# Opening a feed-forward stage with two plain pairs, with the sums of x on VectorE

## The chip, the cores and the metric

The program runs on one core of a Trainium2 chip. The metric is the device time of one execution in microseconds. It is Bass code under the Tile framework: Tile places the buffers and semaphores and orders the instructions of each engine by its own timeline, except inside `strict()` (L102), where TensorE, VectorE and ScalarE instructions keep the order in which the program writes them. GpSimd's do not.

## The reference, cut to what matters

Two layers over 1024 prompt and 32 sample tokens (1056 columns) with model width 1024 and inner width 2816, all in float32. Layer 0 is a gated convolution mixer and layer 1 is attention; each is followed by this feed-forward block, which the change touches:

```python
def _conv_ffn(h, ctx, w_up, conv_w, w_down):
    up = h @ w_up                                  # 1024 -> 2 * 2816
    upc, new_ctx = _causal_dwconv(up, ctx, conv_w) # width 3, along the tokens
    g, v = jnp.split(upc, 2, axis=-1)
    return (jax.nn.silu(g) * v) @ w_down, new_ctx  # h = rmsnorm(x), x is added after
```

## The kernel before, in words

Tokens lie along the free dimension, channels on the 128 partitions: x is 8 tiles of 128 x 1056. A float32 product is made of three passes on TensorE with fp32r operands: each operand is split into a high part (ScalarE copy) and a low part (VectorE subtraction), and high*high, high*low and low*high are summed in PSUM. One matmul has 264 columns.

A feed-forward stage (`ffn`, L811) makes 22 pairs of 128-channel units, g and v of the same channels. From pair 2 on a pair goes by Strassen-Winograd (`pair`, L729): the 1024 x 256 weight and the two halves of the tokens are cut in blocks, and seven products of 24 matmuls (168) take the place of eight (192). It needs sums of the weight blocks (`ws`, four GpSimd operations a pair), the blocks of x named "11", "21" and "22", and the sums of x named t1 to t4, each four tiles with high and low part. Evictions are ScalarE copies and VectorE additions. After each pair `act` does the convolution: per unit a ScalarE product and two VectorE taps, then silu, the product of both and its split (`last`). From pair 3 on, the down projection of two finished pairs is streamed between the products (`stream`, L882).

The opening of a stage is written in strict order. `tokenwise` (L354) ends the stage before, normalising x in four column pieces (ENDS); the last piece's scalings are left to `begin`. `begin` (L531) makes pair 0 plainly, in two halves of the tokens, 96 matmuls each over eight steps, and splits the blocks of x on the way. After each step `tick` runs functions that are due at that step (`at`) and then jobs in order while their costs fit the room (`job`). In the second half it starts the sums: `first` and `second` make them in place in x, one half of each on VectorE and one on GpSimd; t1 to t3 have their low parts from VectorE, t4 from GpSimd. Pair 1 is then a Strassen pair of its own (`first_pair`, L775) whose seven products wait for t1 to t4 in turn, while the convolution of pair 0 is put in as jobs. Then all that is left is emitted, with the whole convolution of pair 1, and Tile's order begins with pair 2. The whole opening happens twice, once per layer.

Buffers: `slot` (14 in a stage), `keep` (24), `w` (4 weight operands), `wr` (5 raw weight blocks), and PSUM banks "p" (3) for the pairs and "d" (2) for the stream.

Of the kernel before, what the change touches and what calls it, by code (L numbers as in the profile page):

```python
# [12 lines left out]
F32 = mybir.dt.float32  # L13
# [15 lines left out]
PAD = 2  # L29
# [12 lines left out]
NF = DFF // 128  # L42
NP = HEADS // 2
SLOTS = 20
UPSLOTS = 14
# [40 lines left out]
class Net:  # L86
# [267 lines left out]
    def tokenwise(self, weight, acts, x, scale, units=(), lag=False):  # L354
# [16 lines left out]
        for c in ENDS:  # L371
# [19 lines left out]
            for k in range(3):  # L391
                self.at(3 + k, lambda f=steps: next(f))
            if c is ENDS[-1]:
                self.norm = scale(c, out[:, cs])
            else:
                for f in scale(c, out[:, cs]):
                    self.job(f, 0.45, 9 if c is ENDS[-2] and units else 7)
# [133 lines left out]
    def begin(self, x, early, late):  # L531
# [5 lines left out]
        one, two = (slice(*c) for c in HALVES)  # L537
        orders = tuple(range(NK)), tuple(k + i for k in range(k2) for i in (0, k2))

        def made(n, k, src, engine=None):  # L540
            def high():
                near = n in ("t2", "t4") or n == "t3" and k < 2
                t = b[n][k] = (self.keep if near else self.slot)("b", [128, 2, HB], F32R)
                self.nc.scalar.activation(t[:, 0], src, AF.Copy)

            def low():
                t = b[n][k]
                (engine or self.nc.vector).tensor_sub(t[:, 1], src, t[:, 0].bitcast(F32))

            return high, low  # L550

        def first(k):
            p, q = x[k], x[k + k2]
            self.nc.vector.tensor_sub(p[:, one], p[:, two], p[:, one])
            self.nc.gpsimd.tensor_sub(p[:, two], q[:, two], p[:, two])

        def second(k):
            q = x[k + k2]
            self.nc.vector.tensor_sub(q[:, two], q[:, two], x[k][:, one])
            self.nc.gpsimd.tensor_sub(q[:, one], q[:, two], q[:, one])  # L560

        t1 = [made("t1", k, x[k][:, one]) for k in range(k2)]
        t2 = [made("t2", k, x[k + k2][:, two]) for k in range(k2)]
        t3 = [made("t3", k, x[k][:, two]) for k in range(k2)]
        t4 = [made("t4", k, x[k + k2][:, one], self.nc.gpsimd) for k in range(k2)]
        for i in range(2):
            c = HALVES[i]
            ps = [self.bank("p").rearrange("p (q c) -> p q c", q=2) for _ in us]
            for n, m in enumerate(orders[i]):
# [16 lines left out]
                if i and n == 4 or not i and n == 0:  # L586
                    next(early)
                self.tick(0.4 if i == 0 or n < 2 else 0.7)
                if i and n % 2:
                    k = n // 2  # L590
                    self.job(lambda k=k: first(k), 0.7)
                    self.job(t1[k][0], 0)
                    if k:
                        self.job(t1[k - 1][1], 0.7)
            for u, p in zip(us, ps):
# [6 lines left out]
        self.ready = []  # L602
        self.job(t1[-1][1], 0.7, label="t1")
        for k in range(k2 + 1):
            if k < k2:
                self.job(lambda k=k: second(k), 0.7)
                self.job(t2[k][0], 0)
            if k:
                self.job(t2[k - 1][1], 0.7, label="t2")
        order = (2, 3, 0, 1)  # L610
        for k, last in zip(order + (None,), (None,) + order):
            if k is not None:
                self.job(t3[k][0], 0)
            if last is not None:
                self.job(t3[last][1], 0.7, label="t3")
        todo = late(us)
        todo = iter([todo[i] for i in (0, 4, 1, 2, 3, 5, 6, 7)])
        for k in range(k2 + 1):
            if k < k2:
                self.job(t4[k][0], 0)  # L620
            if k:
                self.job(t4[k - 1][1], 0, label="t4")
                cost, f = next(todo)
                self.job(f, cost)
        for cost, f in todo:
            self.job(f, cost)
        return b, us

# [145 lines left out]

    def first_pair(self, top, low, b, us):  # L775

        todo = self.pair(top, low, b, us)
        later = todo[4][3]
        todo = [todo[i] for i in (0, 4, 2, 1, 3, 5, 6)]
        for i in (3, 4):  # L780
            todo[i][0]()
        yield
        for _, operand, _, _ in todo[:2]:
            operand(True)
        yield
        for i, (_, _, product, evict) in enumerate(todo):
            self.until({1: "t1", 3: "t2", 4: "t3", 5: "t4"}.get(i))
            product()
            self.tick(1.4)
            if i + 2 < len(todo):  # L790
                if i + 3 == len(todo):
                    todo[-1][0]()
                todo[i + 2][1]()
            if i != 1:
                evict()
            if i == 4:
                later()
            yield

    def late(self, dst, src, ps):  # L800

        for d, q, s in self.cuts():
            self.nc.vector.tensor_add(dst[:, d], src[:, q, s], ps[:, q, s])

    def first(self, l):

        return [self.a["w_up"][l, i] for i in (0, NF)]

    def ffn(self, l, x, done):
# [4 lines left out]
        def act(t, g, v):  # L814

            y = {}

# [5 lines left out]
            def last():  # L823
# [3 lines left out]
                for d, p in spread((0, TT), PAD, PAD):  # L827
                    self.nc.scalar.activation(h[:, d], y[1][:, p], AF.Copy)
                    self.nc.vector.tensor_sub(low[:, d], y[1][:, p], h[:, d].bitcast(F32))  # L829
                acts.append((h, low))  # L830

            todo = ((1.0, lambda: taps(0, g, t)),
                    (1.3, lambda: self.taps(y[0], g, cw[:, t], 1)),
                    (1.3, lambda: self.taps(y[0], g, cw[:, t], 2)),
                    (0.3, lambda: self.nc.scalar.activation(y[0], y[0], AF.Silu)),
                    (1.0, lambda: taps(1, v, NF + t)),
                    (1.3, lambda: self.taps(y[1], v, cw[:, NF + t], 1)),
                    (1.3, lambda: self.taps(y[1], v, cw[:, NF + t], 2)),
                    (2.5, last))
            return todo  # L840

        acts = []
        for t in range(1, NF):
            if t == 1:
                with self.strict():
                    early = self.first_pair(a["w_up"][l, 1], a["w_up"][l, NF + 1], self.b, later)
                    b, us = self.begin(x, early, lambda us: act(0, *us))
                    for _ in early:
                        pass
                self.finish()  # L850
                for _, f in act(1, *later):
                    f()
                fill, n, at, many, lag = iter(()), 0, 0, 4 * NK, 8
                continue
# [5 lines left out]
            for todo in self.pair(a["w_up"][l, t], a["w_up"][l, NF + t], b, us, t == 2):  # L860
                for f in todo:
                    f()
                at += 1
                while n and (many - n) * (14 - lag) < at * many:
                    n -= 1
                    next(fill, None)
            for _, f in act(t, *us):
                f()
            if t % 2:
# [629 lines left out]
```

## Time and profile before

| | |
|---|---|
| median of 3 runs | 2587.91 us (2585.9 to 2588.81) |
| the profiled execution | 2584.78 us |
| its span | 2582.9 us |
| PE, DVE, ACT, POOL busy | 96%, 60%, 47%, 37% of the span |
| mean granted TensorE clock | 0.983 of full speed |

PE is TensorE, DVE VectorE, ACT ScalarE, POOL GpSimd. A matmul's own duration is a latency, since they overlap; what counts is how many start in a stretch. The clock is a share of 2.4 GHz; 0.5 is 1.2 GHz. In strict code every instruction has L72, the line of the helper, so one goes by the names of the tiles.

### The profile page before, as it was taken

To read this page: it belongs to the slowest core of one execution; us is meant where nothing else is said; L and a number is where in the kernel's file an instruction comes from. 1 tells how busy PE (TensorE), PEld (TensorE's weight loads), DVE (VectorE), ACT (ScalarE), POOL (GpSimd) and SP (SyncE) were. 2 spreads that over 40 slices of the span, in tenths; PEclk is the share of its full clock that TensorE was granted. 3 is DMA by queue.
4 is the path that set the end of the run, shared out by engine and by line. 5 is a ranking of instruction groups with operands and counts; after the bars stand their busy time and mean duration, and the time that the engine had idled before them with its cause. 6 is when DMAs were issued, how large, how long until landed. Compare 5 with 4: busy or idle time off the path is not lost. (4 is left out here: it accounts for less than half of the span.)

```text
span 2582.9 us, 47183 instructions
## 1 busy us (share of the span) xinstructions
PE 2482.0 (96%) x18436; PEld 2440.0 (94%) x18436; DVE 1544.6 (60%) x2617; ACT 1219.7 (47%) x2378; POOL 945.6 (37%) x984
## 2 busy tenths in 40 slices
PE   7999998899999999998999999999899999999997
PEld 6999998899999999997999999999899999999996
DVE  5534448855555555665677666765875555555575
ACT  4111114555555555444566666643545555555554
POOL 3000014444444444342454444412544444334423
PEclk9999999899999999998999999999899999999998
DMA  3111122276676666631233332373137676666751
GB/s 109 50 41 50 49 85 74 56 128 117 118 120 117 117 117 117 138 115 49 73 79 79 79 78 75 78 245 100 57 76 124 118 122 115 115 116 118 121 143 68
DMA packets 147631, 254.76 MB, mean 99 GB/s; under 512 B 22352, under 2 KB 58320, under 8 KB 147408
## 3 DMA queue, kind: packets, MB, share of 16 engines
q0 software_dynamic: 41472, 77.88, 22.8%
q1 hardware_dynamic: 105936, 173.87, 22.5%
q8 instruction: 145, 2.38, 0.4%
q14 instruction: 78, 0.64, 0.1%
HBM read 130.52 MB, written 113.04 MB: 94 GB/s over the span
## 5 line engine op out<-in xcount | busy, mean ns | idle before, releaser
L725 PE MATMUL pb_p<-b,wb 128*128 128x264 f32 x6720 | 895.9, 285 | 1.0 <-DVE wb L715 0.6
L725 PEld LDWEIGHTS pb_p<-b,wb 128*128 128x128 f32 x6720 | 851.4, 189 | 1.6 <-DVE wb L715 1.0
L898 POOL DMA_DIRECT2D xd<-xs x288 | 261.0, 908 | 506.4 <-ACT xs L896 505.5
L896 ACT ACTIVATE xs<-pb_d 128x264 f32<-128x264 f32 x576 | 218.2, 387 | 345.1 <-PE pb_d L260 311.0
L260 PE MATMUL pb_d<-acth,wb 128*128 128x264 f32 x1152 | 329.1, 286 | 5.4 <-DVE wb L715 5.4
L258 PE MATMUL pb_d<-acth,wb 128*128 128x264 f32 x1152 | 328.3, 286 | 1.5 <-ACT wb L714 1.5
L259 PE MATMUL pb_d<-actl,wb 128*128 128x264 f32 x1152 | 328.9, 286 | 0.3 <-DVE actl L829 0.3
L258 PE MATMUL pb_d<-xh,wh 128*128 128x384 f32 (+2 forms) x864 | 284.7, 332 | 8.6 <-ACT xh L247 7.8
L259 PE MATMUL pb_d<-xl,wh 128*128 128x384 f32 (+2 forms) x864 | 284.7, 329 | 6.2 <-DVE xl L248 6.2
L260 PE MATMUL pb_d<-xh,wl 128*128 128x384 f32 (+2 forms) x864 | 283.4, 328 | 0.0
L474 DVE SCALAR_TENSOR_TENSOR y<-u,cv,y 128x1058 f32<-128x1058 f32 x184 | 237.4, 1337 | 57.8 <-ACT y L470 57.8
L260 PEld LDWEIGHTS pb_d<-acth,wb 128*128 128x128 f32 x1152 | 217.9, 189 | 5.8 <-DVE wb L715 5.8
L258 PEld LDWEIGHTS pb_d<-acth,wb 128*128 128x128 f32 x1152 | 217.2, 189 | 2.3 <-ACT wb L714 2.0
L259 PEld LDWEIGHTS pb_d<-actl,wb 128*128 128x128 f32 x1152 | 217.6, 189 | 0.8 <-DVE actl L829 0.8
L235 ACT ACTIVATE wh<-wraw 128x1024 fp32r<-128x1024 f32 (+1 forms) x69 | 72.2, 1047 | 259.8 <-PE pb_o L259 125.3
L715 DVE TENSOR_TENSOR wb<-wr,wb 128x512 fp32r<-128x512 f32 x196 | 155.8, 796 | 63.3 <-ACT wb L714 53.3
L715 DVE TENSOR_TENSOR wb<-ws,wb 128x512 fp32r<-128x512 f32 x160 | 124.8, 781 | 96.1 <-ACT wb L714 96.1
L456 POOL COPY u<-cv 128x4 f32<-128x4 f32 x96 | 66.6, 694 | 316.1 <-DVE u L682 256.0
L747 POOL TENSOR_TENSOR ws<-wr 128x512 f32<-128x512 f32 x84 | 125.4, 1493 | 140.6 <-DMA wr<-in_w_up 112.6
L258 PEld LDWEIGHTS pb_d<-xh,wh 128*128 128x128 f32 x864 | 164.4, 191 | 9.7 <-ACT xh L247 8.0
L259 PEld LDWEIGHTS pb_d<-xl,wh 128*128 128x128 f32 x864 | 164.6, 191 | 8.3 <-DVE xl L248 7.9
L260 PEld LDWEIGHTS pb_d<-xh,wl 128*128 128x128 f32 x864 | 164.4, 190 | 0.3
(358 smaller groups left out, 5041.2 us busy)
## 6 DMA issues: line engine op xcount, KB each, us to landing
xd<-xs POOLq DMA_DIRECT2D x288, 264.0 KB, 4.3
wr<-in_w_up SPq DMA_DIRECT2D x168, 256.0 KB
wr<-in_w_down SPq DMA_DIRECT2D x80, 256.0 KB
x<-xd SPq DMA_DIRECT2D x48, 264.0 KB
wraw<-in_w_in SPq DMA_DIRECT2D x23, 512.0 KB
xd<-x SPq DMA_DIRECT2D x64, 132.0 KB
wraw<-in_w_kq SPq DMA_DIRECT2D x16, 512.0 KB
xd<-x SPq DMA_DIRECT2D x16, 264.0 KB
```

The source lines that it names most:

```text
L235: nc.scalar.activation(h[:, i:j], raw[:, i:j], AF.Copy)
L258: nc.tensor.matmul(ps, wh, xh[:, c[0]:c[1]], start=(i == 0), stop=False)
L259: nc.tensor.matmul(ps, wh, xl[:, c[0]:c[1]], start=False, stop=False)
L260: nc.tensor.matmul(ps, wl, xh[:, c[0]:c[1]], start=False, stop=(i == n - 1))
L456: self.nc.gpsimd.tensor_copy(v, st.rearrange("p (a b) -> p a b", b=2))
L474: self.nc.vector.scalar_tensor_tensor(y, u[:, i:i + TC], w[:, i:i + 1], y, op0=OP.mult, op1=OP.add)
L715: nc.vector.tensor_sub(t[:, 1], src, t[:, 0].bitcast(F32))
L725: nc.tensor.matmul(ps[:, q, :QB], w[:, i, k], t[:, j, cs], start=(begin and k == 0 and n == 0), stop=(end and k == len(b) - 1 and n == 2), ...
L747: getattr(self.nc.gpsimd, "tensor_" + op)(dst, x, y)
L896: nc.scalar.activation(t[:, q * QB:(q + 1) * QB], ps, AF.Copy)
L898: nc.gpsimd.dma_start(d, t, accum_op=OP.add)
```

## The change

Pair 1 is made plainly as well, 192 matmuls with no sums of x, evicted by ScalarE alone. All sums of x and all their low parts go to VectorE and are emitted after pair 0's second half. `first_pair` is replaced by `plain`. What is left of pair 0's convolution and that of pair 1 goes into a list, `put_off`, of which two entries are emitted after each product of pair 2; pair 2's goes between the products of pair 3. The square root of the last column piece is asked for one step earlier, and the scalings of the piece before it come in the order in which the second half uses them.

```diff
+LATER = tuple(k + i for k in range(NK // 2) for i in (0, NK // 2))
...
             for k in range(3):
-                self.at(3 + k, lambda f=steps: next(f))
+                self.at((2 if c is ENDS[-1] else 3) + k, lambda f=steps: next(f))
...
+                todo = scale(c, out[:, cs])
+                if c is ENDS[-2] and units:
+                    todo = [todo[i] for i in LATER]
+                for f in todo:
                     self.job(f, 0.45, 9 if c is ENDS[-2] and units else 7)
...
         def first(k):
             p, q = x[k], x[k + k2]
             self.nc.vector.tensor_sub(p[:, one], p[:, two], p[:, one])
-            self.nc.gpsimd.tensor_sub(p[:, two], q[:, two], p[:, two])
+            self.nc.vector.tensor_sub(p[:, two], q[:, two], p[:, two])
 
         def second(k):
             q = x[k + k2]
             self.nc.vector.tensor_sub(q[:, two], q[:, two], x[k][:, one])
-            self.nc.gpsimd.tensor_sub(q[:, one], q[:, two], q[:, one])
+            self.nc.vector.tensor_sub(q[:, one], q[:, two], q[:, one])
...
-                self.tick(0.4 if i == 0 or n < 2 else 0.7)
-                if i and n % 2:
-                    k = n // 2
-                    self.job(lambda k=k: first(k), 0.7)
-                    self.job(t1[k][0], 0)
-                    if k:
-                        self.job(t1[k - 1][1], 0.7)
+                self.tick(0.4)
...
+        sums = [(n, k, x[k + d][:, h]) for n, ks, d, h in (
+            ("t1", range(k2), 0, one), ("t3", (2, 3), 0, two), ("t2", range(k2), k2, two), ("t3", (0, 1), 0, two),
+            ("t4", range(k2), k2, one)) for k in ks]
+        for k in range(k2):
+            self.job(lambda k=k: first(k), 1.4)
+        for k in range(k2):
+            self.job(lambda k=k: second(k), 1.4)
+        todo = [made(*t) for t in sums]
+        for (high, _), (_, low) in zip(todo + [(None, None)], [(None, None)] + todo):
+            if high:
+                self.job(high, 0)
+            if low:
+                self.job(low, 0.7)
+        self.job(lambda: None, 0, label="sums")
+        for f in late(us):
+            self.job(f, 1.2)
+        return b
...
+    def plain(self, top, low, b, us):
+
+        us += [self.slot("u", [128, WID]) for _ in range(2)]
+        raw = [[self.block(src, i) for i in range(2)] for src in (top, low)]
         yield
+        w = [[self.operand(t, True) for t in raw[0]]]
         yield
+        for j, u in enumerate(us):
+            for i in (1, 0):
+                ps = self.bank("p").rearrange("p (q c) -> p q c", q=2)
+                for k in range(2):
+                    self.product(ps, w[j][k], b["12"[k] + "12"[i]], begin=k == 0, end=k == 1)
+                    self.tick(3.0)
+                    if len(w) < 2:
+                        w.append([self.operand(t) for t in raw[1]])
+                for d, q, s in self.cuts() if i else ((slice(PAD, PAD + QB), 0, slice(0, QB)),
+                                                      (slice(PAD + QB, PAD + HB), 1, slice(0, QB))):
+                    self.nc.scalar.activation(u[:, d], ps[:, q, s], AF.Copy)
+                yield
...
-                    early = self.first_pair(a["w_up"][l, 1], a["w_up"][l, NF + 1], self.b, later)
-                    b, us = self.begin(x, early, lambda us: act(0, *us))
+                    early = self.plain(a["w_up"][l, 1], a["w_up"][l, NF + 1], self.b, later)
+                    b = self.begin(x, early, lambda us: act(0, *us))
                     for _ in early:
                         pass
-                self.finish()
-                for _, f in act(1, *later):
-                    f()
+                    self.until("sums")
+                put_off = [j[2] for j in self.jobs] + act(1, *later)
+                self.jobs = []
...
             for todo in self.pair(a["w_up"][l, t], a["w_up"][l, NF + t], b, us, t == 2):
-                for f in todo:
+                for f in todo + tuple(put_off[:2]):
                     f()
+                put_off = put_off[2:]
...
-            for _, f in act(t, *us):
-                f()
+            put_off += act(t, *us)
+            if t > 2:
+                for f in put_off:
+                    f()
+                put_off = []
```

## Rows read from the trace of the kernel before

**Rows 1.** The page's first part: busy time, share of the span, instructions.

```profile
PE 2482.0 (96%) x18436; PEld 2440.0 (94%) x18436; DVE 1544.6 (60%) x2617; ACT 1219.7 (47%) x2378; POOL 945.6 (37%) x984
```

**Rows 2.** Busy time by stretch in layer 0's opening: second half of pair 0, pair 1, pair 2, the start of pair 3, and a later stretch for comparison. Columns: stretch, its length, then busy us (instructions) of PE, PEld, DVE, ACT, POOL, then the granted clock, the DMA share and GB/s.

```profile
423.60:440.20 16.60, 13.66 (x95) 13.24 (x96) 15.98 (x26) 9.04 (x17) 5.38 (x4) 0.90 0.12 33
440.20:467.70 27.50, 20.66 (x132) 19.20 (x130) 22.08 (x23) 15.74 (x30) 21.53 (x17) 0.81 0.07 20
467.70:491.20 23.50, 22.81 (x183) 22.43 (x183) 23.46 (x27) 11.86 (x17) 12.93 (x10) 1.00 0.15 46
491.20:501.30 10.10, 6.34 (x37) 5.84 (x37) 7.48 (x11) 2.59 (x5) 3.56 (x4) 0.83 0.40 93
520.00:540.00 20.00, 20.00 (x166) 20.00 (x165) 9.03 (x14) 10.38 (x20) 11.42 (x14) 1.00 0.82 148
```

**Rows 3.** What TensorE waited for over the whole span: us in total, times, longest.

```profile
PE pb_p L72 <- DVE b L72: 13.8, 10, 3.4
PE pb_d L260 <- DVE wb L715: 5.4, 2, 2.7
PE pb_p L72 <- DVE x L72: 4.1, 3, 1.6
```

**Rows 4.** TensorE in order of time in layer 0's opening: start, us, what, and in brackets the idle time before it and who ended it. The rstd matmul, the end of the first half, the start and end of the second, the start of pair 1, its longest wait, the end of pair 2, the stream's first waits, and the point from which pair 3 runs on.

```profile
415.14 0.56 PE L72 MATMUL pb_d<-ones,acc 128*88 128x1 f32 x6
...
423.27 0.28 PE L72 MATMUL pb_p<-b,wl 128*128 128x264 f32 x1
...
427.81 0.81 PE L72 MATMUL pb_p<-b,wh 128*128 128x264 f32 x2 [0.70 <-ACT u L72]
...
440.33 6.33 PE L72 MATMUL pb_p<-b,wk 128*128 128x264 f32 x48
...
453.51 0.63 PE L72 MATMUL pb_p<-b,wb 128*128 128x264 f32 x3 [3.43 <-DVE b L72]
...
479.72 11.49 PE L725 MATMUL pb_p<-b,wb 128*128 128x264 f32 x93
491.98 0.39 PE L258 MATMUL pb_d<-acth,wb 128*128 128x264 f32 x1 [0.77 <-ACT wb L714]
...
495.41 0.51 PE L260 MATMUL pb_d<-acth,wb 128*128 128x264 f32 x2 [2.67 <-DVE wb L715]
...
501.57 6.02 PE L725 MATMUL pb_p<-b,wb 128*128 128x264 f32 x48
```

**Rows 5.** The same in layer 1's opening: end of the first half, start of pair 1, end of pair 2, the stream's first row, and the point from which pair 3 runs on.

```profile
1830.80 0.28 PE L72 MATMUL pb_p<-b,wl 128*128 128x264 f32 x1
...
1848.48 6.01 PE L72 MATMUL pb_p<-b,wk 128*128 128x264 f32 x48
...
1889.73 8.59 PE L725 MATMUL pb_p<-b,wb 128*128 128x264 f32 x69
...
1908.35 3.92 PE L725 MATMUL pb_p<-b,wb 128*128 128x264 f32 x31
```

**Rows 6.** VectorE in order of time in layer 0's opening: scalings of x beside and away from GpSimd, sums of x, low parts, and the last piece of work before VectorE first falls idle.

```profile
420.78 4.78 DVE L72 SCALAR_TENSOR_TENSOR x<-x,gain,rstd 128x264 f32<-128x264 f32 x4
425.48 0.69 DVE L72 TENSOR_TENSOR b<-x,b 128x528 fp32r<-128x528 f32 x1
426.10 1.29 DVE L72 SCALAR_TENSOR_TENSOR x<-x,gain,rstd 128x264 f32<-128x264 f32 x3
...
432.64 0.70 DVE L72 TENSOR_TENSOR x<-x 128x528 f32<-128x528 f32 x1
433.27 0.69 DVE L72 TENSOR_TENSOR b<-x,b 128x528 fp32r<-128x528 f32 x1
...
437.47 1.82 DVE L72 TENSOR_TENSOR x<-x 128x528 f32<-128x528 f32 x1
...
498.01 0.70 DVE L771 TENSOR_TENSOR u<-u,pb_p 128x528 f32<-128x528 f32 x1
```

**Rows 7.** GpSimd in order of time beside them: the three weight sums of pair 1, and one sum of x.

```profile
420.30 1.72 POOL L747 TENSOR_TENSOR ws<-wr 128x512 f32<-128x512 f32 x1 [8.67 <-DMA wr<-in_w_up]
422.09 1.36 POOL L747 TENSOR_TENSOR ws<-ws,wr 128x512 f32<-128x512 f32 x1
423.41 1.46 POOL L747 TENSOR_TENSOR ws<-wr 128x512 f32<-128x512 f32 x1
...
437.06 1.66 POOL L555 TENSOR_TENSOR x<-x,x 128x528 f32<-128x528 f32 x1 [1.90 <-DVE x L72]
```

**Rows 8.** VectorE by groups from 440.2 to 498.8 us: operation, count, busy us, mean ns, idle before. Low parts of the sums, and the taps (two lines), products and low parts of the first two acts.

```profile
L72 DVE TENSOR_TENSOR b<-x,b 128x528 fp32r<-128x528 f32 x10 | 12.1, 1231 | 0.1
L474 DVE SCALAR_TENSOR_TENSOR y<-u,cv,y 128x1058 f32<-128x1058 f32 x4 | 6.1, 1569 | 0.0
...
L72 DVE SCALAR_TENSOR_TENSOR y<-u,cv,y 128x1058 f32<-128x1058 f32 x4 | 5.8, 1444 | 0.0
...
L824 DVE TENSOR_TENSOR y<-y 128x1058 f32<-128x1058 f32 x2 | 2.5, 1248 | 0.0
L829 DVE TENSOR_TENSOR actl<-y,acth 128x1024 fp32r<-128x1024 f32 x2 | 2.4, 1212 | 0.0
```

**Rows 9.** ScalarE by groups from 440.2 to 467.7 us: high parts, and evictions of a plain product's pieces.

```profile
L72 ACT ACTIVATE b<-x 128x528 fp32r<-128x528 f32 x13 | 8.1, 639 | 9.1 <-DVE x L72 4.9 <-DVE b L72 4.1
...
L72 ACT ACTIVATE u<-pb_p 128x264 f32<-128x264 f32 x2 | 0.8, 384 | 0.0
```

More of the change, by code (lines that the diff above doesn't have):

```diff
@@ L395, in tokenwise @@
             else:
-                for f in scale(c, out[:, cs]):
+                todo = scale(c, out[:, cs])
+                if c is ENDS[-2] and units:
+                    todo = [todo[i] for i in LATER]
+                for f in todo:
                     self.job(f, 0.45, 9 if c is ENDS[-2] and units else 7)
@@ L537, in begin, with made @@
         one, two = (slice(*c) for c in HALVES)
-        orders = tuple(range(NK)), tuple(k + i for k in range(k2) for i in (0, k2))
-        def made(n, k, src, engine=None):
+        orders = tuple(range(NK)), LATER
+        def made(n, k, src):
             def high():
@@ L547, in low @@
                 t = b[n][k]
-                (engine or self.nc.vector).tensor_sub(t[:, 1], src, t[:, 0].bitcast(F32))
+                self.nc.vector.tensor_sub(t[:, 1], src, t[:, 0].bitcast(F32))
             return high, low
@@ L559, in second @@
             self.nc.vector.tensor_sub(q[:, two], q[:, two], x[k][:, one])
-            self.nc.gpsimd.tensor_sub(q[:, one], q[:, two], q[:, one])
[L562 to L565, printed above, removed]
+            self.nc.vector.tensor_sub(q[:, one], q[:, two], q[:, one])
         for i in range(2):
@@ L602, in begin @@
         self.ready = []
[L603 to L627, printed above, removed]
+        sums = [(n, k, x[k + d][:, h]) for n, ks, d, h in (
[15 more added lines that the diff above has]
+        return b
     def norms(self, x, ms):
@@ L773, in pair @@
         )
[L775 to L781, printed above, removed]
+    def plain(self, top, low, b, us):
+        us += [self.slot("u", [128, WID]) for _ in range(2)]
+        raw = [[self.block(src, i) for i in range(2)] for src in (top, low)]
         yield
-        for _, operand, _, _ in todo[:2]:
-            operand(True)
+        w = [[self.operand(t, True) for t in raw[0]]]
         yield
[L786 to L798, printed above, removed]
+        for j, u in enumerate(us):
[10 more added lines that the diff above has]
+                yield
     def late(self, dst, src, ps):
@@ L814, in act @@
         def act(t, g, v):
-            y = {}
+            y, into = {}, acts
             def taps(i, u, t):
@@ L829, in last @@
                     self.nc.vector.tensor_sub(low[:, d], y[1][:, p], h[:, d].bitcast(F32))
[L830 to L840, printed above, removed]
+                into.append((h, low))
+            return [lambda: taps(0, g, t), lambda: self.taps(y[0], g, cw[:, t], 1), lambda: self.taps(y[0], g, cw[:, t], 2),
+                    lambda: self.nc.scalar.activation(y[0], y[0], AF.Silu), lambda: taps(1, v, NF + t),
+                    lambda: self.taps(y[1], v, cw[:, NF + t], 1), lambda: self.taps(y[1], v, cw[:, NF + t], 2), last]
         acts = []
```

## The prediction

> **What bounds the kernel now.** The page's first part comes first: PE is busy 96% of the span, so time can come only out of PE's work or its gaps [rows 1]. The page's slices then show where PE is below nine tenths beside the two ends: at the openings of both feed-forward stages. The busy times by stretch say how much: away from an opening 166 matmuls start in 20 us, 0.1205 us each; in pair 1 only 132 start in 27.5 us, at a granted clock of 0.81 [rows 2]. The list of waits names the releasers: low parts of the sums of x (b, 13.8 us in all), the weight splits of the stream (wb, 5.4 us), the scaled x (4.1 us) [rows 3]. TensorE in order of time then gives three places per opening where time is lost [rows 4, 5]:
>
> (a) Second half of pair 0. The first half's matmuls end at 423.4, the second runs freely only from 427.81, and pair 1 starts at 440.33. Unhindered its 96 matmuls last 96 x 0.1205 = 11.6 us, to 435.1: 5.2 us lost. In layer 1: 1830.9 + 11.6 = 1842.6 against 1848.48, 5.9 lost [rows 4, 5].
>
> (b) Pairs 1 and 2, 14 x 24 = 336 matmuls, 40.5 us. They last from 440.33 to 491.2, 50.9 us, 10.4 too long, and in layer 1 from 1848.48 to 1898.3, 49.8 us, 9.3 too long [rows 4, 5].
>
> (c) The start of pair 3: 14 matmuls of the stream and 24 of pair 3, 4.6 us of work, stand between 491.2 and 501.57, 10.4 us (37 of them are in [rows 2]): 5.8 lost. In layer 1 the same from 1898.3 to 1908.35 loses 5.5 [rows 4, 5]. Here VectorE is late: it is busy all of pair 2 (23.46 of 23.5 us, [rows 2]) and works on without a break to 498.7, 7.5 us past pair 2's end [rows 6].
>
> Sum of the losses: 11.1 (a) + 19.7 (b) + 11.3 (c) = 42.1 us.
>
> **The change part by part.** *The plain pair's matmuls.* 192 for 168 in each layer: 2 x 24 x 0.1205 = 5.8 us of PE's own time, on the path without cover.
>
> *Pair 1's weight sums go.* Three GpSimd sums (420.30 to 424.87, [rows 7]) lie beside four scalings of x that take 4.78 us; three scalings right after take 1.29, 0.43 each [rows 6]. So the four lose about 3.1 us, and PE's second half waits for just these scalings and the low part behind them. Plain has no weight sums, and GpSimd has nothing else to do there. The rstd matmul moves up by one step of 12 matmuls, 1.45 us; it stands at 415.14 now, behind three steps [rows 4]. Together the first low part of the second half, which stands at 425.48, comes some 4 us earlier, at 421.5, before the first half's end at 423.4. From there VectorE needs one scaling and one low part, 0.41 + 0.62 = 1.03 us, for a step of PE that takes 1.45. I count all of (a), 11.1 us; what is late next would be the eviction of pair 0's first bank by ScalarE (0.70, [rows 4]), which no longer queues behind a high part that waits for VectorE. The order LATER and the room of 0.4 cost nothing: VectorE and ScalarE run in program order and reach these jobs by their own pace.
>
> *The sums and low parts on VectorE.* Without GpSimd beside it a sum or a low part takes 0.62 us from start to start (425.48 to 426.10, 432.64 to 433.27), beside it up to 1.82 [rows 6]; the ten low parts after 440.2 had a mean of 1231 ns [rows 8]. 16 sums and 16 low parts, 12 of them GpSimd's before, make 32 x 0.62 = 19.8 us at the free pace and 32 x 1.23 = 39.4 at the loaded one. VectorE's last low part of pair 0 ends at 433.96; less the 3.1 us and less one sum in front of it that's gone, 430; after pair 1's first two weight splits 432. Then 19.8, two more splits (each like a low part, 1.2) and a wait for them that I estimate at 1.4, since their buffers come free at pair 0's end and ScalarE evicts first: 454.4. Pair 2's first three weight sums on GpSimd come next to it, another 3.1 as above: 457.5. PE's plain pair runs from 435.1 to 435.1 + 192 x 0.1205 = 458.2. The first sum that is asked for (t2) is wanted by pair 2's second product, at 458.2 + 2.9 = 461. So the sums lie beside the plain pair. I take the free pace, because GpSimd's own sums and low parts, which loaded it, are what leaves. At the loaded pace they would end near 477, t2 near 470, and pair 2 would wait some 8 us a layer.
>
> The Trainium skill, "SBUF — State Buffer", section "SBUF: two separate sides", has the two engines share a port pair that one of them holds for a whole instruction while the other is blocked. By it the four scalings would lose GpSimd's whole 4.54 us instead of the 3.1 seen, and the sums here would end at 459.0 instead of 457.5, still before 461.
>
> *ScalarE in the plain pair.* 16 high parts of 0.64 and ten eviction pieces of 0.38 are 14 us of 23.1 [rows 9]; the few splits and taps beside them, which it had in pair 1 before too (15.7 us of 27.5 in all, [rows 2]), fit in the rest. The highs wait for sums alone, and all sums come ahead of all low parts, so no eviction waits behind one. Three banks serve products of 48 matmuls, 5.8 us each: nothing.
>
> *SP and buffers.* Eight raw blocks of pairs 1 and 2 are loaded as before, and pair 1's are free sooner. "12" keeps its four slots until the plain pair's sixth product (435.1 + 6 x 2.9 = 452), so that pair 0's first tap waits for that; nobody on PE's path needs it for 30 us.
>
> *(b) after the change*: 360 matmuls, 43.4 us, and a rest at the hand-over to pair 2, whose first weight split now queues on VectorE behind three taps of pair 0. At 1.25 to 1.57 us a tap [rows 8] this is 0 to 4 us; I take 1.2 a layer, one tap ahead of the split. So (b) gives 19.7 - 2.4 = 17.3 before the 5.8.
>
> *Putting the convolutions between products.* Two acts are 17.2 us of VectorE [rows 8] and stay so. VectorE ends now 30.9 us after pair 2's start (467.8 to 498.7). Of this leave the additions that evict pair 1 (about 2.5), some two taps done beside the plain pair (2.5), and the neighbourhood of GpSimd's low parts (about 3): 23 us, to 458.2 + 23 = 481, against pair 2's end at 458.2 + 20.2 + 1.2 = 479.6. So the lateness falls from 7.5 to about 1.5 us. A wait costs more than itself, as PE restarts at a lower clock (waits of 0.77 and 2.67 stand behind the 5.8 lost, [rows 4]), so I leave 3 us of (c) in each layer; bounds are 0 (splits always ahead of taps) and all 5.8, or more if the list is ordered worse (a rival below). (c) gives 11.3 - 6 = 5.3.
>
> Sum: 11.1 + 17.3 + 5.3 - 5.8 = 27.9 us, 28. The profiled execution becomes 2584.8 - 28 = 2557; the median lies 3.1 above it, so 2560.
>
> **The rivals.**
> *VectorE stays the bound after pair 1.* It is busy 60% over the span but wholly so in pair 2 [rows 1, 2], and its work between pair 0 and pair 3 hardly shrinks. Then (c) stays whole (-5.3) and pair 2 waits 2 us more a layer (-4): gain 18 to 19, 2569. For: 7.5 us of lateness. Against: the first 8 sums and 4 low parts were GpSimd's at 1.7 us each and slowed VectorE beside them.
>
> *The sums are late.* If VectorE's loaded pace holds without GpSimd's sums, pair 2 waits 8 us a layer: gain 28 - 16 = 12, 2576. Against: 0.43 against 1.2 us for the same scaling within 6 us [rows 6].
>
> *The second half of pair 0 isn't GpSimd's doing.* Then (a) stays: 28 - 11 = 17, 2571. Against: the slow scalings end where the weight sums end, at 425.5 and 424.9 [rows 6, 7].
>
> *Slower: taps ahead of each weight split.* Two entries of the list are emitted between two products of pair 2, and VectorE was full there before [rows 2]. If they stand ahead of the next product's split, PE waits before each product, and such gaps bring its clock to 1.2 GHz: pair 1, with waits up to 3.43 us, had a mean grant of 0.81 [rows 2, 4]. At the lower level throughout, pair 2's 168 matmuls last 40.5 us instead of 20.2: 20.2 lost a layer where I left 1.2, so 28 - 38 = -10: 2598. It decides from 15.2 us lost in a pair 2 (1.2 + 28 / 2). Against: in the old pair 2, with VectorE as full, the grant was 1.00 [rows 2], and its splits went between the taps of two acts.
>
> **How the numbers follow.** Forecast 58%, own range 2552 to 2568 (the upper end of the gain is all losses less the plain matmuls, 42.1 - 5.8 = 36.3). VectorE bound 20%, sums late 7%, (a) stays 4%, slower 8%, nothing of note 3%. The range goes from 2550 to 2577 and leaves out mainly the slower case and the worse half of late sums. About 0.2%, 5 us, is what a measurement of this kernel can tell from no change. Faster: 58 + 20 + 4 + 5 = 87%; same: 3 + 2 = 5%; slower 8%.
>
> **What would show it.** In the changed profile the second half of pair 0 should follow the first without a gap, at a granted clock of 1.0, and end near 435; the scalings there should take 0.41 to 0.43 each. The plain pair should last 23 us without a wait for b. VectorE should be through the sums by 458. The waits for wb of the stream should shrink from 2.7 us to about 1 us. It would be wrong if PE waits for b in pair 2 (sums late), or if the stretch behind pair 2 is longer than 10 us (acts late).

## The result and the profile after

The changed kernel takes 2549.70 us (median of 4 runs, 2549.31 to 2550.09), the kernel before 2587.62 beside it (2585.9 to 2588.81): a ratio of 0.9854 [0.9837, 0.9871], 37.9 us less. The forecast was 2560 with a range of 2550 to 2577: the direction was right, the gain was 10 us larger than forecast, and the time lies 0.3 us below the range. The profiled executions stand at 2584.78 and 2550.09, 34.7 apart. One further execution of the kernel before, beside the second group of kernels below, took 11785.65 us; the ratios and ranges leave it out.

The page's first part after, against [rows 1]: PE has 48 matmuls more and is busy 10 us less; a matmul at a lower clock is busy longer, and such stretches are gone.

```profile
PE 2471.9 (97%) x18484; PEld 2433.1 (95%) x18484; DVE 1531.6 (60%) x2617; ACT 1216.5 (48%) x2388; POOL 899.3 (35%) x952
```

Busy time by stretch in layer 0's opening, columns as in [rows 2]: first half of pair 0, second half, plain pair 1, pair 2 with the first product of pair 3, and the stream's start.

```profile
411.70:424.40 12.70, 12.64 (x104) 12.60 (x105) 10.30 (x25) 5.60 (x13) 0.77 (x1) 1.00 0.45 139
424.40:436.50 12.10, 12.01 (x98) 11.80 (x98) 11.77 (x21) 5.93 (x12) 0.00 (x0) 1.00 0.15 45
436.50:459.90 23.40, 23.40 (x194) 23.40 (x193) 21.66 (x28) 12.77 (x29) 10.59 (x10) 1.00 0.13 46
459.90:484.50 24.60, 23.78 (x194) 23.57 (x194) 23.69 (x28) 16.17 (x26) 10.39 (x8) 1.00 0.15 44
484.50:500.00 15.50, 15.50 (x130) 15.50 (x129) 14.74 (x19) 9.91 (x18) 3.74 (x4) 1.00 0.38 76
```

The granted clock is 1.00 in all five; before it was 0.90, 0.81 and 0.83 in three of the stretches [rows 2]. VectorE is as full as it was (21.7 of 23.4 us, 23.7 of 24.6), and PE hardly waits for it. TensorE in order of time, against [rows 4, 5]; the last row is from layer 1:

```profile
436.53 11.91 PE L73 MATMUL pb_p<-b,wk 128*128 128x264 f32 x96
448.27 11.86 PE L73 MATMUL pb_p<-b,wb 128*128 128x264 f32 x96
459.97 14.84 PE L711 MATMUL pb_p<-b,wb 128*128 128x264 f32 x120
475.63 9.04 PE L711 MATMUL pb_p<-b,wb 128*128 128x264 f32 x72 [0.82 <-ACT u L753]
484.51 0.28 PE L259 MATMUL pb_d<-acth,wb 128*128 128x264 f32 x1
...
485.00 3.10 PE L711 MATMUL pb_p<-b,wb 128*128 128x264 f32 x24
487.93 0.41 PE L261 MATMUL pb_d<-acth,wb 128*128 128x264 f32 x2
...
490.60 0.40 PE L259 MATMUL pb_d<-acth,wb 128*128 128x264 f32 x2
...
491.57 0.29 PE L260 MATMUL pb_d<-actl,wb 128*128 128x264 f32 x1
...
1864.80 9.03 PE L711 MATMUL pb_p<-b,wb 128*128 128x264 f32 x72 [0.96 <-ACT u L753]
```

The plain pair lasts 436.53 to 459.97, 23.4 us. In each opening one wait is left from here to the stream, for an eviction by ScalarE (0.82 and 0.96). In the list of waits the rows for b (13.8 us) and for the stream's wb (5.4) of [rows 3] are gone; the 4.1 us for x stay:

```profile
PE pb_p L73 <- DVE x L73: 4.1, 3, 1.6
...
PE pb_p L711 <- ACT u L753: 1.8, 2, 1.0
```

The losses counted before, 42.1, less the plain pair's 5.8, less the 1.8 us of waits that are left, make 34.5; the two profiled executions differ by 34.7. That the two agree is luck, because the 42.1 rests on a wrong count. Part (b) of the prediction puts 336 matmuls, all of pairs 1 and 2, between 440.33 and 491.2. Pair 1's 168 are there, but of pair 2's (L725) only 144 in either layer; its last product runs behind the stream's first chains. Columns: stretch, its length, busy us of PE with L725 alone (instructions), the granted clock, the DMA share and GB/s:

```profile
440.33:491.20 50.87, 18.23 (x144) 0.90 0.11 32
1848.48:1898.30 49.82, 18.13 (x144) 0.86 0.10 33
```

[rows 2] say the same: 132 + 183 = 315 start in a stretch that is slightly wider. So each layer lost 24 x 0.1205 = 2.9 us more than booked, 47.9 in all. Measured from the first matmul of one opening to that of the next, and from there to the end, the changed kernel is 18.4 and 17.3 us shorter (1407.5 and 764.7 us before, 1389.1 and 747.4 after), and its first opening begins 1.1 us later (411.76 against 410.69). Those 35.7 us are some 5 less than 47.9 - 5.8 - 1.8; new waits of the stream for ScalarE's copies (xs, 1.6 us in four) are part of that, and the rest I can't place.

VectorE in order of time, against [rows 6]: scalings, first sum of x, the last low part, an eviction by addition (L755) that frees a bank of pair 2, a weight split for the stream, and the end of the second act:

```profile
421.42 1.70 DVE L73 SCALAR_TENSOR_TENSOR x<-x,gain,rstd 128x264 f32<-128x264 f32 x4
...
432.10 0.70 DVE L73 TENSOR_TENSOR x<-x 128x528 f32<-128x528 f32 x1
...
461.34 0.70 DVE L73 TENSOR_TENSOR b<-x,b 128x528 fp32r<-128x528 f32 x1
...
476.62 0.69 DVE L755 TENSOR_TENSOR u<-mid,pb_p 128x528 f32<-128x528 f32 x1
...
482.99 1.45 DVE L701 TENSOR_TENSOR wb<-wr,wb 128x512 fp32r<-128x512 f32 x1
...
489.32 1.31 DVE L810 TENSOR_TENSOR actl<-y,acth 128x1024 fp32r<-128x1024 f32 x2
```

The four scalings that took 4.78 take 1.70. The sums begin at 432.10 and end at 462.0. Most important are the last three rows. Pair 2's seven products and pair 3's first, the 120 and 72 matmuls above, are through at 484.5, and the act of pair 1, the second act, only at 490.6, 6 us later. PE doesn't wait for it, for two reasons. The eviction at L755 stands 13 us ahead of its end, so PE gets its bank in time. And TensorE's own order puts matmuls of pair 3 between those of the stream's first chains: the stream's first matmul on a low part of weights is at 487.93 (the split ends at 484.4), and the first on the second act are at 490.60 (high part) and 491.57 (low part), 1 us behind its end.

The sums and low parts by groups, VectorE from 431 to 462 us (columns as in [rows 8]): 25.4 us in all for the 32.

```profile
L73 DVE TENSOR_TENSOR b<-x,b 128x528 fp32r<-128x528 f32 x16 | 11.2, 758 | 0.2
L73 DVE TENSOR_TENSOR x<-x 128x528 f32<-128x528 f32 x8 | 7.6, 949 | 0.1
L73 DVE TENSOR_TENSOR x<-x,x 128x528 f32<-128x528 f32 x8 | 6.6, 840 | 0.1
```

### The profile page after: what moved, and what is told of

The parts are those of the page before. It is cut to its first block, busy times and chain, and to the rows that moved or that the text cites. A ratio compares the mean times of both kernels' runs of the same rounds, so it can differ in the third digit from the quotient of the medians.

```text
span 2548.3 us, 47227 instructions
## 1 busy us (share of the span) xinstructions
PE 2471.9 (97%) x18484; PEld 2433.1 (95%) x18484; DVE 1531.6 (60%) x2617; ACT 1216.5 (48%) x2388; POOL 899.3 (35%) x952
```

## The experiments

Every run was timed beside the kernel before on the same chip, whose medians were 2587.71, 2587.22 and 2586.26 in three groups of kernels. "Against after" means against 2549.70.

### Where the convolutions stand

**All that is put off emitted at once, ahead of pair 2.**

```diff
-                put_off = [j[2] for j in self.jobs] + act(1, *later)
-                self.jobs = []
+                for f in [j[2] for j in self.jobs] + act(1, *later):
+                    f()
+                put_off, self.jobs = [], []
...
-            if t > 2:
+            if t > 1:
```

> The changed kernel with its convolutions in the old places: what is left of pair 0's and the whole of pair 1's are emitted before pair 2, pair 2's after it. Theory A (the order in which TensorE's instructions stand, which follows the list, puts products of pair 3 between the stream's chains, so that it need not wait for the second act): the waits at the start of pair 3 come back, 5.8 and 5.5 us, so about 11 us slower than the changed kernel, near 2561. Theory B (VectorE simply has less work after pair 1 and is in time whatever the list): under 2 us slower, 2550 to 2552.

2564.34 us (2561.63 to 2568.54), 0.9911 [0.9897, 0.9924] of before: 14.6 more than after. Theory A held, with a somewhat larger price. TensorE of this kernel at the stream's start, then VectorE's weight split that it waits for:

```profile
479.93 0.39 PE L259 MATMUL pb_d<-acth,wb 128*128 128x264 f32 x1 [0.77 <-ACT wb L700]
...
483.31 0.81 PE L261 MATMUL pb_d<-acth,wb 128*128 128x264 f32 x2 [2.63 <-DVE wb L701]
485.57 0.81 PE L259 MATMUL pb_d<-acth,wb 128*128 128x264 f32 x2 [1.45 <-ACT acth L809]
486.83 0.59 PE L260 MATMUL pb_d<-actl,wb 128*128 128x264 f32 x1 [0.45 <-DVE actl L810]
...
487.88 10.95 PE L711 MATMUL pb_p<-b,wb 128*128 128x264 f32 x72
```

```profile
482.58 0.68 DVE L701 TENSOR_TENSOR wb<-wr,wb 128x512 fp32r<-128x512 f32 x1
```

The waits of [rows 4] at the stream are back (0.77 and 2.63, there 0.77 and 2.67). They are for a weight split of the stream and for the second act (acth, actl). VectorE is no later with either than in after: the split ends at 483.3 (there 484.4), the second act at 487.5 (there 490.6). What differs is that TensorE's chains stand ahead of pair 2's last product and of pair 3, with nothing between their matmuls. L755 also runs later, at 486.69 instead of 476.62, since both acts now stand ahead of it on VectorE, but here PE is held up by the chains, not by that. The waits add up to 5.3 us, but the loss is larger, since the granted clock falls with them. The same 20 us of both kernels, columns as in [rows 2], this one first (the profiled run is its longest), then after:

```profile
480.00:500.00 20.00, 15.47 (x95) 14.64 (x96) 11.63 (x19) 7.45 (x12) 6.21 (x6) 0.74 0.21 48
```

```profile
480.00:500.00 20.00, 20.00 (x167) 20.00 (x166) 19.25 (x24) 11.01 (x19) 6.30 (x7) 1.00 0.30 60
```

72 matmuls are missing, 8.7 us at 0.1205 each, at a grant of 0.74.

**The list alone, on the kernel before.** Strassen pair 1, sums on GpSimd as before, only the convolutions go between later products:

```diff
-                self.finish()
-                for _, f in act(1, *later):
-                    f()
+                while self.due:
+                    self.tick(0)
+                self.until("t4")
+                put_off = [j[2] for j in self.jobs] + [f for _, f in act(1, *later)]
+                self.jobs = []
...
-                for f in todo:
+                for f in todo + tuple(put_off[:2]):
                     f()
+                put_off = put_off[2:]
...
```

> The kernel before with nothing changed but the list: after the sums, what is left of pair 0's convolution and that of pair 1 go two by two between the products of pair 2, pair 2's between those of pair 3. Theory A (order of TensorE): the losses at the start of pair 3 go, about 11 us faster than the kernel before, near 2576. Theory B (work of VectorE): VectorE is as late as before, no gain, 2585 to 2589.

2574.06 us (2572.49 to 2574.46), 0.9945 [0.9932, 0.9959]: 13.6 less than before, a little over the 11.3 booked as (c). TensorE runs from pair 2 into pair 3 and the stream without a wait (first fence), while the list of waits still has those for b (second):

```profile
476.80 23.56 PE L725 MATMUL pb_p<-b,wb 128*128 128x264 f32 x192
500.20 0.28 PE L258 MATMUL pb_d<-acth,wb 128*128 128x264 f32 x1
```

```profile
PE pb_p L72 <- DVE b L72: 14.0, 11, 3.4
```

So the list removes the waits of (c) by itself, with VectorE no less full than before: 23.4 of these 23.4 us. Here too the stream's first chain stands behind all of pair 2.

**Is it the place of the stream's chains on PE instead?** In the first of these kernels the stream's first chain follows 144 of pair 2's 168 matmuls, in after all 168 and 24 of pair 3. This kernel keeps the flush and moves the stream two products later:

```diff
-                fill, acts, n, at = self.stream(a["w_down"][l, t - 2:t], acts), [], many, -lag
+                fill, acts, n, at = self.stream(a["w_down"][l, t - 2:t], acts), [], many, -lag - (2 if t == 2 else 0)
```

> The kernel of e1_flush (old places of the convolutions, which was 14.6 us slower than the changed kernel), with the stream asked for two products later. VectorE has the same work in the same list order as in e1_flush; only the stream's first chains stand 4 products behind, after pair 3's fourth product instead of ahead of pair 2's last. Theory A (the place of the chains on TensorE is what costs): the waits at pair 3 go, 2549 to 2553. Theory B (VectorE's order, with whole convolutions ahead of the weight splits, is what costs): the splits of pair 3's own products are late instead, 2558 to 2565.

2575.89 us (2574.61 to 2578.54), 0.9960 [0.9948, 0.9973]: neither number, and 11.6 worse than the flush alone. The first chains no longer wait for weights or acts; the product that follows pair 2's first 144 matmuls waits, for a bank. TensorE, then VectorE:

```profile
487.41 16.35 PE L711 MATMUL pb_p<-b,wb 128*128 128x264 f32 x120 [8.39 <-DVE u L755]
```

```profile
486.57 0.70 DVE L755 TENSOR_TENSOR u<-mid,pb_p 128x528 f32<-128x528 f32 x1
```

A bank of pair 2 comes free only when L755 has read it, and L755 still stands behind both acts. Theory A (the chains' place alone) falls; of theory B the order on VectorE holds, but an eviction is late, not a weight split. The 8.4 us a layer and 120 matmuls at a lower clock behind them (16.2 us, where 14.5 is the full pace) are most of the 26.2 us against after; the list of waits has 6.5 us more, in four, for ScalarE's copies in the stream (xs).

So the list does two things at once. On VectorE it puts pair 2's evictions ahead of the second act; without that, moving PE's work only exchanges one wait for another (this run). On TensorE it leads to an order with matmuls of pairs 2 and 3 ahead of and between the stream's chains; with the chains in their old place PE waits although VectorE is no later (the first run above). No run has the list's order on VectorE with the chains in their old place. That this would wait too is argued from the times of the split and of the second act.

**Three entries of the list per product instead of two.**

```diff
-                for f in todo + tuple(put_off[:2]):
+                for f in todo + tuple(put_off[:3]):
                     f()
-                put_off = put_off[2:]
+                put_off = put_off[3:]
```

> The changed kernel with three entries of the list after each product of pair 2 instead of two, so that pair 1's convolution is done with pair 2's sixth product. Theory A (the evictions and splits of a pair must stand ahead of the convolutions on VectorE; the eviction that stood at 476.6 in the changed kernel and at 486.6 in e8_flush_late moves back): part of the loss returns, 2551 to 2560. Theory B (only whole convolutions ahead of everything hurt): 2549 to 2551.

2549.32 us (2548.52 to 2551.41), 0.9857 [0.9842, 0.9873]: the same as after. It decides nothing between the theories, since the third entry didn't move what it was to move: up to 495 us VectorE's instructions come in the same order as in after, L755 at 476.10 and the end of the second act at 490.1, in an execution that runs 0.5 us ahead. All that it shows is that Tile makes much the same order of two entries and of three.

### The plain pair and the sums

**Only the sums on VectorE, on the kernel before.**

```diff
-            self.nc.gpsimd.tensor_sub(p[:, two], q[:, two], p[:, two])
+            self.nc.vector.tensor_sub(p[:, two], q[:, two], p[:, two])
...
-        t4 = [made("t4", k, x[k + k2][:, one], self.nc.gpsimd) for k in range(k2)]
+        t4 = [made("t4", k, x[k + k2][:, one]) for k in range(k2)]
```

> The kernel before with all sums of x and t4's low parts on VectorE and nothing else changed. Theory A (GpSimd beside VectorE costs VectorE as much as it spares it): within 4 us of the kernel before, 2583 to 2591, as the waits for b in pair 1 change places. Theory B (VectorE alone is much faster): 5 to 10 us faster, 2577 to 2583.

2585.40 us (11 runs, 2583.71 to 2586.37), 0.9994 [0.9985, 1.0003]: no difference that can be told, as theory A had it.

**All but the plain pair:** the kernel before with the list and with the sums on VectorE, by the two diffs above, and with the earlier step and LATER. Pair 1 stays a Strassen pair, and the sums keep their order in `begin`.

```diff
-                self.at(3 + k, lambda f=steps: next(f))
+                self.at((2 if c is ENDS[-1] else 3) + k, lambda f=steps: next(f))
...
-                for f in scale(c, out[:, cs]):
+                todo = scale(c, out[:, cs])
+                if c is ENDS[-2] and units:
+                    todo = [todo[i] for i in LATER]
+                for f in todo:
...
```

> All of the change but the plain pair: pair 1 stays a Strassen pair (5.8 us less of TensorE's own time), with its sums on VectorE, the list, the earlier square root and the new order. Theory A (the plain pair is the cover that the sums need, and it takes the weight sums away from the scalings): (a) stays at 11 us and waits for b in pair 1 stay at 10 or more, so 2568 to 2578. Theory B (VectorE's pace alone was the trouble): 2550 to 2560.

2571.36 us (2570.77 to 2572.6), 0.9942 [0.9929, 0.9954]. In the list of waits those for b stand as before:

```profile
PE pb_p L73 <- DVE b L73: 15.3, 10, 3.4
```

Theory A. So the plain pair, with the weight sums that it makes needless and the order of the sums that it allows, is worth 21.7 us, and the rest of the change doesn't remove the waits for b.

**The sums back on GpSimd, in the changed kernel** (one of two sums in `first` and in `second`, and t4's low parts).

```diff
-                self.nc.vector.tensor_sub(t[:, 1], src, t[:, 0].bitcast(F32))
+                (self.nc.gpsimd if n == "t4" else self.nc.vector).tensor_sub(t[:, 1], src, t[:, 0].bitcast(F32))
...
-            self.nc.vector.tensor_sub(p[:, two], q[:, two], p[:, two])
+            self.nc.gpsimd.tensor_sub(p[:, two], q[:, two], p[:, two])
...
-            self.nc.vector.tensor_sub(q[:, one], q[:, two], q[:, one])
+            self.nc.gpsimd.tensor_sub(q[:, one], q[:, two], q[:, one])
```

> The changed kernel with half of the sums of x and t4's low parts back on GpSimd. Theory A (the cover of the plain pair is enough, whoever makes the sums): up to 2 us slower, 2549 to 2552. Theory B (the move to VectorE is needed, since GpSimd's 12 operations of 1.7 us also hold up VectorE's beside them): the sums end some 8 us later, t4 after pair 2's sixth product, waits for b come back in pair 2: 5 to 16 us slower, 2555 to 2566.

2557.61 us (2556.86 to 2560.94), 0.9886 [0.9872, 0.9899]: 7.9 more than after, theory B. PE doesn't wait for a b, though, but for an eviction. TensorE, then ScalarE:

```profile
465.64 6.12 PE L711 MATMUL pb_p<-b,wb 128*128 128x264 f32 x48 [2.12 <-ACT u L73]
472.63 6.10 PE L711 MATMUL pb_p<-b,wb 128*128 128x264 f32 x48 [0.88 <-DVE mid L752]
```

```profile
464.33 0.64 ACT L73 ACTIVATE b<-x 128x528 fp32r<-128x528 f32 x1 [1.38 <-POOL b L552]
464.88 0.71 ACT L73 ACTIVATE u<-pb_p 128x264 f32<-128x264 f32 x3
```

The high parts wait on ScalarE for GpSimd, and the plain pair's evictions (u<-pb_p, 464.88) queue behind them. So the price is within theory B's numbers by another wait than it named. The same move of the sums is worth 1.8 us (not told from none) on the kernel before and 7.9 on top of the plain pair and the list.

### The second half of pair 0

**Pair 1's weight sums back.** The changed kernel with three GpSimd additions and subtractions of the raw weights in `plain`, which nothing reads:

```diff
+        s1, s2, s3 = (self.slot("ws", [128, NK // 2, 128], F32, "ws", 3) for _ in range(3))
+        self.nc.gpsimd.tensor_add(s1, raw[1][0], raw[1][1])
+        self.nc.gpsimd.tensor_sub(s2, s1, raw[0][0])
+        self.nc.gpsimd.tensor_sub(s3, raw[0][0], raw[1][0])
```

> The changed kernel with three GpSimd sums of pair 1's raw weights, read by nobody, where the old pair 1 had its weight sums. Theory A (they, beside the scalings of x, are what held up the second half of pair 0): four scalings take over 4 us again instead of 1.7, TensorE waits some 2 us before the second half and runs at the lower clock after it: 3 to 5 us a layer, 2556 to 2560. Theory B (the earlier square root is what closed that gap): within 1 us a layer, 2550 to 2552.

2559.65 us (2556.74, 2556.77, 2562.52, 2562.82), 0.9891 [0.9878, 0.9905]: 7 to 13 more than after, the median within theory A's numbers. GpSimd, then VectorE beside it, then the waits of TensorE that follow:

```profile
419.21 1.33 POOL L766 TENSOR_TENSOR ws<-wr 128x512 f32<-128x512 f32 x1 [7.62 <-DMA wr<-in_w_up]
420.61 1.35 POOL L767 TENSOR_TENSOR ws<-ws,wr 128x512 f32<-128x512 f32 x1
421.93 1.74 POOL L768 TENSOR_TENSOR ws<-wr 128x512 f32<-128x512 f32 x1
```

```profile
419.31 1.52 DVE L73 SCALAR_TENSOR_TENSOR x<-x,gain,rstd 128x264 f32<-128x264 f32 x1
420.75 1.78 DVE L73 TENSOR_TENSOR b<-x,b 128x528 fp32r<-128x528 f32 x1
422.46 2.72 DVE L73 SCALAR_TENSOR_TENSOR x<-x,gain,rstd 128x264 f32<-128x264 f32 x4
```

```profile
425.18 0.39 PE L73 MATMUL pb_p<-b,wh 128*128 128x264 f32 x1 [1.00 <-ACT b L73]
425.92 0.40 PE L73 MATMUL pb_p<-b,wh 128*128 128x264 f32 x1 [0.36 <-DVE b L73]
...
427.50 0.51 PE L73 MATMUL pb_p<-b,wh 128*128 128x264 f32 x2 [0.70 <-ACT u L73]
```

These three groups of VectorE take 6.0 us, against some 2.9 without GpSimd beside them (0.48 and 0.70 just before, and 1.70 for the four in after): 3.1 lost, the prediction's figure. That the gap of [rows 4] returns with them shows that the weight sums made it. By the Trainium skill ("SBUF — State Buffer", section "SBUF: two separate sides") one engine blocks the other for its whole instruction. GpSimd's three last 4.4 us together, and 3.8 even at 1.27 us each, the shortest of the weight sums in after, so the rule overstates the loss here as it did at [rows 6, 7].

**The square root at its old step**, alone (run twice) and together with the weight sums.

```diff
-                self.at((2 if c is ENDS[-1] else 3) + k, lambda f=steps: next(f))
+                self.at(3 + k, lambda f=steps: next(f))
```

> The changed kernel with the last piece's square root asked for at the old step. Theory A (the weight sums held up the second half; the earlier step gives slack): VectorE's scalings come up to 1.4 us later, the second half waits at most 1 us a layer, perhaps with the lower clock behind it: 2549.5 to 2554. Theory B (the step is what closed the gap): 4 us or more a layer, over 2557.

> The kernel of e4_rstd again, whose four runs lay at 2549.9, 2552.7, 2556.4 and 2556.4 with mean granted clocks of 0.990, 0.988, 0.986 and 0.986, and whose profiled run was the fastest of them. Theory A (a wait of 0.5 us a layer lets the clock fall in some runs and not in others): times again between 2549.5 and 2557 in steps of some 3 us, each with its clock, and if the profiled run is a long one, a stretch below 1.00 behind the first half's end. Theory B (the spread came from that chip's day): all within 1 us.

> The changed kernel with both edits of pair 0's second half taken back: the three GpSimd sums of raw weights, read by nobody, and the square root at the old step. Theory A (the two together make up the loss (a) of 11.1 us): 2558 to 2563. Theory B (the weight sums alone make it up, and e3_weight_sums, 10 us, already showed it): 2556 to 2560, no more than e3_weight_sums.

Alone it takes 2554.54 us (2549.87, 2552.71, 2556.36, 2556.39), 0.9873 [0.9859, 0.9886], and again 2551.72 (2550.2, 2550.57, 2552.87, 2553.04), 0.9866 [0.9849, 0.9884]. The first median is 0.5 us above theory A's range and below theory B's; the second is within theory A's. In the profiled run (2549.87) it brings one wait an opening (0.55 in layer 1):

```profile
424.04 0.51 PE L73 MATMUL pb_p<-b,wh 128*128 128x264 f32 x2 [0.51 <-ACT u L73]
```

Together with the weight sums it takes 2558.60 us (2557.77 to 2559.99), 0.9892 [0.9877, 0.9908]: no more than the weight sums alone, as theory B had it, though the number lies in both theories' ranges. The earlier step gives some slack, worth 4.8 and 2.0 us by the medians of the two runs without the weight sums, and nothing that can be seen beside them. The same stretch of the weight sums' profiled run, then of both together:

```profile
424.00:437.00 13.00, 10.95 (x85) 10.36 (x84) 12.93 (x25) 6.76 (x12) 0.00 (x0) 1.00 0.13 41
```

```profile
424.00:437.00 13.00, 10.46 (x69) 9.95 (x69) 12.93 (x24) 6.75 (x12) 0.47 (x1) 0.87 0.13 38
```

In the first the three waits add up to 2.1 us and the clock stays at 1.00; in the second to 2.5 us, and it falls to 0.87: 16 matmuls fewer in 13 us, 1.9 us, of which the longer waits are 0.5. In layer 1 the waits are 2.7 and 2.5 us, and the grant of 1813 to 1830 us is 0.90 in both.

**The order of the scalings taken back.**

```diff
                 todo = scale(c, out[:, cs])
-                if c is ENDS[-2] and units:
-                    todo = [todo[i] for i in LATER]
```

> The changed kernel with the scalings of the last piece but one in the old order of x. Theory A (VectorE goes through them in its own order long before they are read, so the order is worth nothing): 2549 to 2551. Theory B (the order is what lets the second half follow at once): TensorE waits 0.5 us or more a layer, and the clock may fall behind that: 2551 to 2557.

2549.91 us (2548.91 to 2553.61), 0.9863 [0.9845, 0.9881]: the order is worth nothing that can be measured, as forecast.

## Why the prediction was right in direction and short in size

**(a), right.** All 11.1 us were booked, and the second half now follows the first without a gap: 98 matmuls start in 12.1 us at a grant of 1.00. From the first matmul of the opening to pair 1 the two layers are 4.9 and 5.5 us shorter, 10.4 in all. With the weight sums alone the kernel loses 7 to 13 again. The sign forecast, scalings of 0.41 to 0.43, is there (1.70 for four).

**The plain pair as cover, right.** It lasts 23.4 us (forecast 23.1), without a wait for b. The sums began when forecast (432.1 for 432) and ended 4.5 us later (462.0 for 457.5): the 32 sums and low parts took 25.4 us where 19.8 and 3.1 beside GpSimd were booked, and three weight splits of pair 2 among them (some 0.7 each) were not booked. The t2 low parts, which come before the last, were still in time. The rival of late sums didn't come.

**(b), mis-sized by a count.** "Pairs 1 and 2, 14 x 24 = 336 matmuls" should have been 312, as shown above: (b) lost 13.3 + 12.2 = 25.5 us and not 19.7, and the prediction took 491.2 for pair 2's end while its last product still stood behind the stream. The rest booked at the hand-over to pair 2, 2.4 us, is close to the 1.8 us of waits that are left, but by luck: they are for ScalarE's eviction, not for a weight split behind taps.

**(c), the step that failed.** "So the lateness falls from 7.5 to about 1.5 us ... so I leave 3 us of (c) in each layer." The second act ends 6 us behind pair 2, so VectorE is later than forecast, and PE doesn't wait for it at all. I took the time at which VectorE ends its backlog for the time at which PE gets what it asks for. What counts is what stands ahead of L755 on VectorE and what stands ahead of the stream's chains on TensorE; the list changes both, and takes nothing from VectorE's work. The two kernels with the flush show it: with the chains early PE waits for the split and the second act (14.6 us more), with the chains late for L755, at 486.6 instead of 476.6 (26.2 more). The list alone gives 13.6.

The sum (27.9) missed the profiled gain (34.7) by 6.8. The 6.0 us left in (c) and the 5.8 not counted in (b) are 11.8 too little; against them stand the 0.7 missing in (a), the first opening's later start, 1.1, and the waits in the stream that the prediction didn't have.

**The step from the profiled execution to the median, also mis-sized.** I carried the 3.1 us between before's profiled execution (2584.78) and its median over to the changed kernel. After's profiled execution is its longest run, 0.4 above its median. Before's profiled execution happened to be shorter than all of its timed runs (2585.3 to 2590.4 in the three groups), so the offset was that one execution's. Nor did the spread go with the waits: after's four runs lie within 0.8 us, but those of the kernel with the old order of the scalings, whose profile shows no other waits there, within 4.7.

**The rivals.** The slower case didn't come: pair 2 has a grant of 1.00 and one wait of 0.8 us. That (a) wasn't GpSimd's doing is refuted by the weight sums. That VectorE stays the bound was half true: it is as full as before, and PE no longer waits for it here.

The parts don't add up one by one: the list alone 13.6, the sums on VectorE alone 1.8 (not told from none), all but the plain pair 15.9, and the plain pair 21.7 on top.

## What to carry to other kernels

When an engine in the middle runs late, ask in its program order what stands ahead of the instruction that the bottleneck waits for, and in the bottleneck's own order what it can do before it needs the result; the end of the backlog is neither time. Count the matmuls of a stretch in the trace before pricing what it lost. Price the parts of a change together where one of them only provides cover, as the plain pair does for the sums of x. And compare profile with profile and median with median: an offset between the two of one kernel needn't hold for the other.

## What the runs showed of the hardware

GpSimd beside VectorE is dear here: three GpSimd operations on raw weights made six VectorE instructions beside them 3.1 us longer, and through them the kernel 7 to 13 us.

Executions of one kernel differ, and the mean granted clock follows. With the square root at its old step the first four runs took 2549.87 to 2556.39 us, 0.990 in the shortest and 0.986 in the longest; with the weight sums 2556.74 to 2562.82, 0.988 and 0.986. Short waits in pair 0's second half needn't be the reason: the kernel with the old order of the scalings, whose profiled run has none there, took 2548.91 to 2553.61, 0.990 and 0.986. In the profiled runs with the weight sums, waits of 2.1 us in all left the clock at 1.00, and waits of 2.5 to 2.7 us came with 0.87 and 0.90. What decides the clock in a given run stays open; the long runs of these kernels were not profiled.
